# RWKV products over all 128 rows, adaLN weights as the moving operand, and shared accumulator buffers in a hybrid trunk kernel

## The chip, the core and the metric

The kernel runs on one core of a Trainium2 chip. A core has a matrix engine (TensorE, "PE" in the profile), a vector engine (VectorE, "DVE"), a scalar engine (ScalarE, "ACT"), a general engine (GpSimd, "POOL") and a queue engine that issues transfers (SyncE, "SP"). Each engine carries out its own instructions in order, and engines wait for each other through semaphores. Matmuls write to PSUM, which has eight banks, each 512 float32 values in each of 128 rows; everything else lies in SBUF. The metric is device time in microseconds (us). A comparison uses the median of several runs.

## What is computed

Two layers with shared weights go over 1,024 latent tokens and 256 context tokens of width 1,024. Three parts matter here.

```
mod = silu(c) @ w_ada[l] + b_ada[l]         # adaLN: 6 x 1024 columns per layer, for c and for c_ctx
h   = rmsnorm(x) * (1 + scale) + shift
...
w_raw = w0 + tanh(wd) @ w2                  # RWKV, per direction d; the two inputs are 64 wide
a     = sigmoid(a0 + ad @ a2)
S     = S * w_t + (S @ -kk_t) (kk_t * a_t) + v_t k_t      # scan over time, 8 heads of 64, two directions
y_t   = S @ r_t
```

The first layer runs attention and the RWKV scan as parallel head groups, the second a Fourier mixing; both end in a gated MLP with a width-3 convolution.

## The kernel before

Everything is float32. Large products split both operands in a high and a low part and add three products (L144 to L146); small ones run in plain float32, which PE carries out as two rows in the trace for each matmul.

The program goes through: the first adaLN blocks and norm, projections and attention, the RWKV part, the output product, the first MLP, the Fourier layer, and the second MLP. The change concerns the RWKV part and the adaLN products.

**RWKV.** The scan is chunked: 64 tokens a chunk, 256 tokens (4 chunks) a round for each direction, five rounds (four for the latent tokens, one for the context). A round has two halves of four heads. A half has four units, one for each direction `d` and pair of heads `pp_`. `unit_values` makes a unit's decays, keys and masks: two `lora` products (L789), then a chain through ACT, POOL and DVE. `unit_products` makes its 64-by-64 matrices (`G_ps`, L926) and transposes (`fl_ps`, L782). `half_prep` alternates the two, so that the products of a unit come behind the values of the next. `inverses` turns the triangular matrices of a whole round into inverses in 31 dependent steps on DVE (L978, L982). `corrections` applies them: `mq_ps` (L1018), `gv_ps` (L1023), `ms_ps` (L1030), `tb_ps` (L1036). `chains` carries the state over four chunks (`ch`, `y_ps`). `post` normalizes the result.

In `mq_ps` and `ms_ps` a matmul uses 32 rows and 32 columns of the array, in `gv_ps` 64 and 64, in `lora_ps` 64 rows and 128 columns. All other products of the part use all 128 rows. The operands stand on the rows that belong to the direction, and nothing is read on the others.

**adaLN.** `ada_steps` makes the first four blocks of 512 columns at the start: the vector is the stationary operand (32 columns, of which 2 hold data), the weights move, and four column quarters of the array (`ps[32 * q:...]`) take four parts of the sum; a second small product with `sel` (L202) adds the quarters and turns the row into columns. The other 10,240 columns are made by `ada_columns` in the RWKV part: the weights are the stationary operand, 128 by 128, and the vector moves with 2 columns (L239), eight matmuls for 128 columns, 80 such groups.

**PSUM in the RWKV part.** Two banks for the state chain `c0`, `c1`, two for `y0`, `y1`, two under the tag `t` for the corrections, two under the tag `g` for preparation, adaLN and `post` (`ps_g`).

**Order.** The function `run` interleaves generators by numbers: `A1` to `A5` say how many adaLN steps go into each phase of a round. The order on each engine is then settled by a scheduler when the program is built, so that instructions stand earlier or later than they are written where no dependence holds them.

Of the kernel before, what the change touches and what calls it, by code (L numbers as in the profile page):

```python
# [30 lines left out]
C = 64  # L31
QB = 6
# [66 lines left out]
def hybrid_step(ctx: ExitStack, tc: tile.TileContext, i: dict, o: dict):  # L99
# [77 lines left out]
    def ada_steps(l, j, wp, pp, tag, nb, kn, wb, sb):  # L177

        part, k1 = j // 2, j % 2 * 4
        ps = pp.tile([128, 512], F32, tag=tag, bufs=nb, name="ada_ps")  # L180
        for k0 in range(0, KD, kn):
            w = wp.tile([128, kn, 512], F32, tag="ada_w", bufs=wb, name="ada_w")
            ada_load[0] = nc.sync.dma_start(
                out=w,
                in_=i["w_ada"][l, k0 * 128:(k0 + kn) * 128, j * 512:(j + 1) * 512].rearrange(
                    "(k p) c -> p k c", p=128
                ),
            )
            for k in range(kn):
                q = (k0 + k) % 4  # L190
                nc.tensor.matmul(
                    ps[32 * q:32 * q + 32], lhsT=csil[:, k0 + k, :], rhs=w[:, k, :],
                    start=(k0 < 4), stop=(k0 >= 4),
                )
            if (k0 + kn) % 2 == 0:
                yield
        mp = wp.tile([128, 4, 128], F32, tag="ada_mp", bufs=sb, name="ada_mp")
        nc.scalar.copy(mp.rearrange("p k c -> p (k c)"), ps)
        yield
        ps = pp.tile([128, 4, 2], F32, tag=tag, bufs=nb, name="ada_ps2")  # L200
        for e in range(4):
            nc.tensor.matmul(ps[:, e, :], lhsT=mp[:, e, :], rhs=sel, start=True, stop=True)  # L202
        bc = lambda t: t.unsqueeze(1).to_broadcast([128, 2, 4])
        m = modc[l][:, part, :, k1:k1 + 4]
        nc.vector.tensor_tensor(
            out=m, in0=ps.rearrange("p k c -> p c k"), in1=bc(bcol[:, l, 4 * j:4 * j + 4]), op=ALU.add
        )
        gi = {1: 0, 2: 1, 4: 2, 5: 3}.get(part)
        if gi is not None:
            nc.vector.scalar_tensor_tensor(  # L210
                out=m, in0=m, scalar=1.0 if part in (1, 4) else 0.0, in1=bc(gcol[:, l, gi, k1:k1 + 4]),
                op0=ALU.add, op1=ALU.mult,
            )
        yield
        if part in (2, 5) and k1:
# [10 lines left out]

    def ada_columns(parts, wp, wb, ps_tile):

        for l, part in parts:
            m = modc[l][:, part]  # L230
            for k1 in range(KD):
                c0 = part * D + k1 * 128
                w = wp.tile([128, KD, 128], F32, tag="ada_c", bufs=wb, name="ada_c")
                nc.sync.dma_start(
                    out=w, in_=i["w_ada"][l, :, c0:c0 + 128].rearrange("(k p) c -> p k c", p=128)
                )
                ps = ps_tile()
                for k in range(KD):
                    nc.tensor.matmul(ps, lhsT=w[:, k, :], rhs=csil[:, k, 0:2], start=(k == 0), stop=(k == KD - 1))  # L239
                nc.scalar.activation(  # L240
                    m[:, :, k1], ps, AF.Identity, bias=bcol[:, l, part * KD + k1:part * KD + k1 + 1]
                )
                if k1 == KD - 1:
                    gi = {1: 0, 2: 1, 4: 2, 5: 3}.get(part)
                    if gi is not None:
                        nc.vector.scalar_tensor_tensor(
                            out=m, in0=m, scalar=1.0 if part in (1, 4) else 0.0,
                            in1=gcol[:, l, gi].unsqueeze(1).to_broadcast([128, 2, KD]), op0=ALU.add, op1=ALU.mult,
                        )
                    if part in (2, 5):  # L250
                        ps = ps_tile([16, 128])
                        nc.tensor.transpose(ps, m.rearrange("p c k -> p (c k)"), ident)
                        row = wp.tile([16, 128], F32, tag="ada_row", bufs=1, name="ada_row")
                        nc.scalar.copy(row, ps)
                        nc.gpsimd.dma_start(out=mod_d[l][part // 3].rearrange("c (k p) -> (c k) p", p=128), in_=row)
                yield
# [110 lines left out]
    with ExitStack() as st:  # L367
# [11 lines left out]
        with ExitStack() as st2:  # L379
# [3 lines left out]
            for _ in ada_blocks([(0, j) for j in (2, 3, 0, 1)], xp, pp, "t", 3, 2, 8, 1):  # L383
                pass
# [315 lines left out]
    with ExitStack() as st:  # L700
# [10 lines left out]
        PG = [pool(st_d, "pg", space=PSUM, side="right"), "g"]  # L711
# [28 lines left out]
        A1, A2, A3, A4, A5 = 5, 2, 3, 2, 8  # L740
# [14 lines left out]
        for t_ in bds + tzs:  # L755
# [12 lines left out]
        def ps_g(shape, name):  # L768
            return PG[0].tile(shape, F32, tag=PG[1], bufs=2, name=name)

# [14 lines left out]
        def lora(H, pp_, d, which, out):  # L785
# [4 lines left out]
                ps, lhsT=H["w"][HS[d], which, pp_ * 128:pp_ * 128 + 128], rhs=H["src"][HS[d], which, :],  # L790
# [4 lines left out]
        def half_new(n):  # L795
# [7 lines left out]
            H["w"] = ep.tile([128, 2, 256], F32, tag="w2", bufs=1, name="w2")  # L803
            for e, nm in enumerate(("rwkv_w2", "rwkv_a2")):
                for d in range(2):
                    nc.sync.dma_start(out=H["w"][HS[d], e, :], in_=i[nm][0, d, :, hf * 256:(hf + 1) * 256])
# [143 lines left out]
        def half_prep(R, H):  # L950
            H["src"] = R["src"]
            last = None
            for d, pp_ in UNITS:
# [1012 lines left out]
```

## Time and profile before

| | |
|---|---|
| median of 3 runs | 3950.23 us (3940.7 to 3959.45) |
| profiled execution | 3953.97 us, its span 3952.2 us |
| mean granted PE clock | 0.905 |
| RWKV part, about 700 to 1720 us of the span | PE busy 912 of 1020 us |
| memory traffic | 75 GB/s over the span |

How to read it: a row of a group names the line, the engine, the operation and its tiles (out<-in), the array's rows and columns in use (32*32), the moving operand's shape, the count, the busy time in us and the mean of one in ns, and then the idle time before them with what ended it. Busy spans of matmuls overlap, since a matmul starts before the one ahead has drained; so how often PE can start one is read from rows in order of time. PEclk is the share of the full PE clock that was granted.

### The profile page before, as it was taken

How to read it: one execution, taken by the hardware profiler on the slowest of the kernel's cores; microseconds unless marked ns; L12 is line 12 of the kernel's file. 1: busy time of each engine (PE TensorE's matmuls, PEld its weight loads, DVE VectorE, ACT ScalarE, POOL GpSimd, SP SyncE). 2: the span in 40 equal slices, each digit the busy share in tenths (PEclk: the TensorE clock that was granted, in tenths of full speed). 3: DMA queues.
4: the chain of work that ended last, by engine and by line, in shares of the span. 5: the costliest groups of instructions: out<-in, count | busy, mean ns of one | idle time of the engine just before them, and what ended most of it. 6: DMA issues, size and time to landing. Idle time of an engine off the chain costs nothing.

```text
span 3952.2 us, 54932 instructions
## 1 busy us (share of the span) xinstructions
PE 3702.0 (94%) x21512; PEld 3137.2 (79%) x21512; DVE 1945.5 (49%) x3685; ACT 1351.6 (34%) x2867; POOL 713.2 (18%) x1180
## 2 busy tenths in 40 slices
PE   7999997789999999789999999999887999999998
PEld 5888886578888878678888888888766888888886
DVE  4377666454444544566444444445655244444445
ACT  4266566533333333245321211212444321112121
POOL 3111111533333243224200000002233000000002
PEclk8999999568686757699999999999898999999999
DMA  6232312223332222144411111111541111111103
GB/s 215 85 100 77 99 65 66 78 78 96 96 100 83 83 81 68 44 144 123 126 40 40 38 34 37 43 38 60 191 125 54 38 38 38 38 40 40 39 30 125
DMA packets 368724, 299.42 MB, mean 76 GB/s; under 512 B 52939, under 2 KB 321067, under 8 KB 368465
## 3 DMA queue, kind: packets, MB, share of 16 engines
q1 hardware_dynamic: 304112, 235.81, 19.7%
q0 software_dynamic: 15952, 40.46, 3.0%
q10 hardware_dynamic: 48400, 19.65, 2.0%
q8 instruction: 169, 2.77, 0.3%
q14 instruction: 91, 0.74, 0.1%
HBM read 239.55 MB, written 58.33 MB: 75 GB/s over the span
## 4 chain that ended last, share of the span: by engine, by line
PE 82%; DVE 5%; DMA 3%; ACT 2%; POOL 2%; issue 2%; ACTq 0%; DVEq 0%; SPq 0%; POOLq 0%
PE a_ps L145 10%; PE a_ps L146 10%; PE a_ps L144 10%; PE b_ps L145 5%; PE b_ps L144 5%; PE b_ps L146 5%; PE ada_ps L239 4%; PE G_ps L926 3%; PE tb_ps L1036 3%; PE f_ps L144 2%; PE f_ps L146 2%; PE f_ps L145 2%; PE pv_ps L590 2%; PE sc_ps L554 2%; PE lora_ps L789 2%
## 5 line engine op out<-in xcount | busy, mean ns | idle before, releaser
L144 PE MATMUL a_ps<-hh,f_hi 128*128 128x512 f32 (+1 forms) x2144 | 761.4, 356 | 18.4 <-ACT f_hi L139 14.8
L145 PE MATMUL a_ps<-hl,f_hi 128*128 128x512 f32 (+1 forms) x2144 | 762.1, 356 | 3.2 <-POOL hl L342 3.2
L146 PE MATMUL a_ps<-hh,f_lo 128*128 128x512 f32 (+1 forms) x2144 | 760.8, 355 | 0.2 <-DVE f_lo L140 0.2
L1381 DVE TENSOR_TENSOR acc<-b_ps,acc 128x512 f32<-128x512 f32 x400 | 270.4, 689 | 405.9 <-PE b_ps L146 405.8
L144 PEld LDWEIGHTS a_ps<-hh,f_hi 128*128 128x128 f32 x2144 | 404.4, 189 | 82.7 <-ACT f_hi L139 15.4
L145 PEld LDWEIGHTS a_ps<-hl,f_hi 128*128 128x128 f32 x2144 | 404.3, 189 | 68.6 <-POOL hl L342 5.2
L146 PEld LDWEIGHTS a_ps<-hh,f_lo 128*128 128x128 f32 x2144 | 404.9, 189 | 63.0 <-DVE f_lo L140 0.9
L145 PE MATMUL b_ps<-d_lo,mh 128*128 128x512 f32 x880 | 349.1, 397 | 0.0
L146 PE MATMUL b_ps<-d_hi,ml 128*128 128x512 f32 x880 | 347.6, 395 | 0.0
L144 PE MATMUL b_ps<-d_hi,mh 128*128 128x512 f32 x880 | 342.1, 397 | 3.6 <-DVE acc L1381 3.1
L1327 POOL MEMSET gp<- 128x1 f32 x44 | 4.3, 98 | 1571.3 <-DVE cv L1346 1571.3
L140 DVE TENSOR_TENSOR f_lo<-f_raw,f_hi 128x512 fp32r<-128x512 f32 x176 | 114.3, 690 | 308.1 <-ACT f_hi L139 305.7
L239 PEld LDWEIGHTS ada_ps<-csil,ada_c 128*128 128x128 f32 x1280 | 218.9, 264 | 22.7 <-ACT th L793 8.5
L239 PE MATMUL ada_ps<-csil,ada_c 128*128 128x2 f32 x1280 | 223.3, 303 | 3.5 <-DMA ada_c<-in_w_ada 2.4
L139 ACT CAST d_hi<-d_raw 128x512 fp32r<-128x512 f32 x88 | 54.5, 621 | 488.5 <-PE b_ps L146 474.9
L144 PEld LDWEIGHTS b_ps<-d_hi,mh 128*128 128x128 f32 x880 | 165.8, 188 | 45.0 <-DVE acc L1381 4.6
L144 PE MATMUL f_ps<-hh,w_hi 128*128 128x512 f32 (+1 forms) x552 | 198.6, 360 | 0.5 <-ACT nk L478 0.5
L146 PEld LDWEIGHTS b_ps<-d_hi,ml 128*128 128x128 f32 x880 | 165.4, 188 | 40.7
L146 PE MATMUL f_ps<-hh,w_lo 128*128 128x512 f32 (+1 forms) x552 | 197.4, 358 | 0.0
L145 PE MATMUL f_ps<-hl,w_hi 128*128 128x512 f32 (+1 forms) x552 | 197.4, 358 | 0.0
L145 PEld LDWEIGHTS b_ps<-d_lo,mh 128*128 128x128 f32 x880 | 165.5, 188 | 37.4
L1338 ACT COPY gp<-a_ps 128x512 f32<-128x512 f32 (+1 forms) x134 | 68.0, 507 | 338.7 <-PE a_ps L146 338.7
(566 smaller groups left out, 6993.6 us busy)
## 6 DMA issues: line engine op xcount, KB each, us to landing
f_raw<-in_w_ffn_in SPq DMA_DIRECT2D x176, 256.0 KB, 3.2
ada_c<-in_w_ada SPq DMA_DIRECT2D x80, 512.0 KB, 4.0
d_raw<-in_w_ffn_out SPq DMA_DIRECT2D x88, 256.0 KB, 2.9
nx<-x_d SPq DMA_DIRECT2D x24, 512.0 KB, 4.6
w_raw<-in_w_in_even SPq DMA_DIRECT2D x23, 512.0 KB, 4.1
rx<-x_d SPq DMA_DIRECT2D x20, 512.0 KB, 7.0
ada_w<-in_w_ada SPq DMA_DIRECT2D x16, 512.0 KB, 8.8
fb_d<-fsh POOLq DMA_DIRECT2D x15, 512.0 KB, 3.1
```

Of the source, the lines that this page charges most:

```text
L140: nc.vector.tensor_tensor(out=lo, in0=src, in1=hi, op=ALU.subtract)
L144: nc.tensor.matmul(ps, lhsT=a[0], rhs=b[0], start=first, stop=False)
L145: nc.tensor.matmul(ps, lhsT=a[0], rhs=b[1], start=False, stop=False)
L146: nc.tensor.matmul(ps, lhsT=a[1], rhs=b[0], start=False, stop=last)
L239: nc.tensor.matmul(ps, lhsT=w[:, k, :], rhs=csil[:, k, 0:2], start=(k == 0), stop=(k == KD - 1))
L554: nc.tensor.matmul(ps[:, :nn], lhsT=qs[:, m, a, :], rhs=ks[m][:, n0:n0 + nn], start=(a == 0), stop=(a == 1),)
L590: nc.tensor.matmul(pv, lhsT=wt[:, kb, :], rhs=vt[:, kb, :], start=(kb == 0), stop=(kb == nk // 128 - 1))
L789: nc.tensor.matmul(ps, lhsT=H["w"][HS[d], which, pp_ * 128:pp_ * 128 + 128], rhs=H["src"][HS[d], which, :], start=True, stop=True,)
L926: nc.tensor.matmul(ps[:, c, :], lhsT=bd[:, c, h, :], rhs=kr[:, c].rearrange("p a s -> p (a s)"), start=True, stop=True,)
L1036: nc.tensor.matmul(ps[:, e, h, :], lhsT=tz[:, c + e, h, :], rhs=g[:, c + e, h, 64:192], start=True, stop=True,)
L1338: nc.scalar.copy(gp[:, o0:o0 + n], up(ws, t0, n))
L1381: nc.vector.tensor_tensor(out=acc[j][:, cs], in0=ps, in1=acc[j][:, cs], op=ALU.add)
```

## The change

Four things change. (1) `lora`, `mq_ps`, `gv_ps` and `ms_ps` read all 128 rows; the rows that hold nothing of the direction are zero in one of the operands, in tiles that are zeroed once (`w2s`, `svs`, `mqs`), and `tz` is zeroed in part in each unit. (2) `ada_columns` is gone; all 12,288 columns go through `ada_steps`, in blocks of 256 columns, with loads of four 128-row parts. (3) `half_prep` makes the values of both directions and then the products of both. (4) The tag `t` is gone: corrections share the tag `g`, now of three banks, with preparation and `post`, and adaLN has one bank of its own. The numbers `A1` to `A5` are set for the new count of steps (five a block, 40 blocks).

```diff
-    def ada_steps(l, j, wp, pp, tag, nb, kn, wb, sb):
+    def ada_steps(l, j, wp, pp, tag, nb, wb, sb):
+        na = AW // 128
+        part, k1 = j * na // KD, j * na % KD
+        ps = pp.tile([128, AW], F32, tag=tag, bufs=nb, name="ada_ps")
+        for k0 in range(0, KD, 4):
+            w = wp.tile([128, 4, AW], F32, tag="ada_w", bufs=wb, name="ada_w")
...
+            for q in range(4):
                 nc.tensor.matmul(
+                    ps[32 * q:32 * q + 32], lhsT=csil[:, k0 + q, :], rhs=w[:, q, :], start=(k0 == 0), stop=(k0 > 0),
                 )
...
-    def ada_columns(parts, wp, wb, ps_tile):
...
-                for k in range(KD):
-                    nc.tensor.matmul(ps, lhsT=w[:, k, :], rhs=csil[:, k, 0:2], start=(k == 0), stop=(k == KD - 1))
...
-            for _ in ada_blocks([(0, j) for j in (2, 3, 0, 1)], xp, pp, "t", 3, 2, 8, 1):
+            for _ in ada_blocks([(0, j) for j in (4, 5, 6, 7, 0, 1, 2, 3)], xp, pp, "t", 3, 8, 1):
...
-        PG = [pool(st_d, "pg", space=PSUM, side="right"), "g"]
+        PG = [pool(st_d, "pg", space=PSUM, side="right"), 3]
...
-        A1, A2, A3, A4, A5 = 5, 2, 3, 2, 8
+        A1, A2, A3, A4, A5 = 18, 4, 6, 6, 16
...
+        w2s = ep.tile([128, 2, 2, 256], F32, name="w2s")
+        svs = [lt.tile([128, NCP, 128], F32, name=f"sv{j}") for j in range(2)]
+        mqs = [lt.tile([128, 8, 32], F32, name=f"mqs{d}") for d in range(2)]
+        for t_ in [w2s] + bds + tzs + svs + mqs:
             nc.gpsimd.memset(t_, 0.0)
...
-                ps, lhsT=H["w"][HS[d], which, pp_ * 128:pp_ * 128 + 128], rhs=H["src"][HS[d], which, :],
+                ps, lhsT=H["w"][:, d, which, pp_ * 128:pp_ * 128 + 128], rhs=H["src"][:, which, :],
...
-            for d, pp_ in UNITS:
-                tmp = unit_values(H, d, pp_)
-                yield
-                if last:
-                    unit_products(R, H, *last, seen)
+            for pp_ in range(2):
+                tmp = []
+                for d in range(2):
+                    tmp.append(unit_values(H, d, pp_))
                     yield
+                for d in range(2):
+                    unit_products(R, H, d, pp_, tmp[d], seen)
+                    yield
...
+                nc.gpsimd.memset(tv[sr, :, fr], 0.0)
...
-                ps = pp.tile([64, nn_, 32], F32, tag="t", bufs=2, name="mq_ps")
+                ps = ps_g([64, nn_, 32], "mq_ps")
...
-                    nc.tensor.matmul(ps[sr, n, :], lhsT=gv[fr, n, sr], rhs=tv[fr, n, fr], start=True, stop=True)
+                    nc.tensor.matmul(ps[:, n, :], lhsT=gv[:, n, 0:64], rhs=tv[:, n, fr], start=True, stop=True)
...
-                            pv[:, c, h, :], lhsT=g[64:128, c, h, 0:64], rhs=sv[:, c, HS[h]], start=True, stop=True
+                            pv[:, c, h, :], lhsT=g[:, c, h, 0:64], rhs=sv[:, c, HS[h]], start=True, stop=True
...
-                    nc.tensor.matmul(ps[sr, n, :], lhsT=tn[sr, :, n0 + n], rhs=qs[sr, n, :], start=True, stop=True)
+                    nc.tensor.matmul(ps[sr, n, :], lhsT=tn[:, :, n0 + n], rhs=qs[:, n, :], start=True, stop=True)
...
-        ada = ada_columns(
-            [(0, 2), (0, 3), (0, 4), (0, 5)] + [(1, a) for a in range(6)], ep, 2, lambda s=[128, 2]: ps_g(s, "ada_ps")
+        ada = ada_blocks(
+            [(0, j) for j in range(8, 24)] + [(1, j) for j in range(24)], ep, PG[0], "ada", 1, 2, 1
         )
...
-                PG[:] = [pp, "t"]
+                PG[:] = [pool(st, "pz", space=PSUM), 2]
```

The built programs show how this moves instructions. On PE, in the preparation ahead of the first inverses, the kernel before has one unit's `lora` products (L789), then the products of the unit ahead of it (`G_ps`), and no adaLN:

```order
L926 MATMUL G_ps<-kr,bd_7297 128x128 x8
L775 MATMUL bon_ps<-bonk,ta 128x2 x2
L782 MATMUL fl_ps<-ident,bkw 128x128 x4
L775 MATMUL kk_ps<-bones,sq 128x2 x2
L782 MATMUL fl_ps<-ident,v 128x128 x2
L782 MATMUL fl_ps<-ident,rsx 128x128 x2
L789 MATMUL lora_ps<-lo_in,w_7649 128x256 x2
L926 MATMUL G_ps<-kr,bd_7296 128x128 x8
```

At the same place the changed kernel (its lines are numbered anew: L760 is `lora`, L897 `G_ps`, L191 the adaLN product with moving weights, L200 the small one with `sel`) has the `lora` products of two units, then the products of the two, and adaLN between them:

```order
L760 MATMUL lora_ps<-lo_in,w2s 128x256 x2
L191 MATMUL ada_ps<-ada_w,csil 32x256 x4
L746 MATMUL kk_ps<-bones,sq 128x2 x2
L753 MATMUL fl_ps<-ident,v 128x128 x2
L200 MATMUL ada_ps_9922<-sel,ada_mp 128x2 x2
L191 MATMUL ada_ps<-ada_w,csil 32x256 x4
L753 MATMUL fl_ps<-ident,rsx 128x128 x2
L760 MATMUL lora_ps<-lo_in,w2s 128x256 x2
L191 MATMUL ada_ps<-ada_w,csil 32x256 x4
L200 MATMUL ada_ps_10002<-sel,ada_mp 128x2 x2
L191 MATMUL ada_ps<-ada_w,csil 32x256 x4
L897 MATMUL G_ps<-kr,bd_7351 128x128 x8
```

adaLN has moved forward: of its 40 blocks of 256 columns in the RWKV part, 21 stand on PE ahead of the first corrections, and all 40 ahead of the second round's. Before, 6 of 80 groups stood ahead of the first corrections, 26 ahead of the second round's, and the last ahead of the fifth round's.

On PE at the first corrections, the kernel before:

```order
L239 MATMUL ada_ps<-csil,ada_c 128x2 x16
L1018 MATMUL mq_ps<-tz_7298,G 32x32 x8
L1023 MATMUL gv_ps<-sv,G 64x64 x8
L926 MATMUL G_ps<-kr,bd_7296 128x128 x4
L1030 MATMUL ms_ps<-mqs,xn 32x32 x8
L926 MATMUL G_ps<-kr,bd_7296 128x128 x4
L775 MATMUL bon_ps<-bonk,ta 128x2 x2
L1036 MATMUL tb_ps<-G,tz_7298 64x128 x8
```

The changed kernel there (L988 is `mq_ps`, L993 `gv_ps`, L1000 `ms_ps`, L1006 `tb_ps`):

```order
L988 MATMUL mq_ps<-tz_7352,G 64x32 x8
L993 MATMUL gv_ps<-sv_7355,G 64x64 x8
L191 MATMUL ada_ps<-ada_w,csil 32x256 x8
L1000 MATMUL ms_ps<-mqs_7357,xn 32x32 x8
L200 MATMUL ada_ps_11389<-sel,ada_mp 128x2 x2
L1006 MATMUL tb_ps<-G,tz_7352 64x128 x8
```

`mq_ps` fills 64 columns of the array where it filled 32, and the work between the corrections is adaLN instead of a unit's products. Counted over PE's rows from the first `kk_ps` to the output product, the shape in use (rows and columns of the array) changes 500 times before and 363 times now.

On ACT at the program's start, the kernel before copies the adaLN sums (`ada_mp`) and squares the input tiles (`njk`) in this order:

```order
L198 COPY ada_mp<-ada_ps 128x512 x3
L295 ACTIVATE njk,nss<-nx 128x1024 x3
L198 COPY ada_mp<-ada_ps 128x512
L295 ACTIVATE njk,nss<-nx 128x1024 x3
```

The changed kernel (L196 is the copy, L262 the square):

```order
L196 COPY ada_mp<-ada_ps 128x256 x5
L262 ACTIVATE njk,nss<-nx 128x1024
L196 COPY ada_mp<-ada_ps 128x256
L262 ACTIVATE njk,nss<-nx 128x1024 x3
L196 COPY ada_mp<-ada_ps 128x256
L262 ACTIVATE njk,nss<-nx 128x1024 x3
L196 COPY ada_mp<-ada_ps 128x256
```

The last copy stands behind seven squares instead of three.

More of the change, by code (lines that the diff above doesn't have):

```diff
@@ L31 @@
 C = 64
+AW = 256
 QB = 6
@@ L175, in hybrid_step @@
     ada_load = [None]
-    def ada_steps(l, j, wp, pp, tag, nb, kn, wb, sb):
[L179 to L182, printed above, removed]
+    def ada_steps(l, j, wp, pp, tag, nb, wb, sb):
[4 more added lines that the diff above has]
+            w = wp.tile([128, 4, AW], F32, tag="ada_w", bufs=wb, name="ada_w")
@@ L183, in ada_steps @@
             ada_load[0] = nc.sync.dma_start(
                 out=w,
-                in_=i["w_ada"][l, k0 * 128:(k0 + kn) * 128, j * 512:(j + 1) * 512].rearrange(
-                    "(k p) c -> p k c", p=128
-                ),
-            )
-            for k in range(kn):
-                q = (k0 + k) % 4
+                in_=i["w_ada"][l, k0 * 128:(k0 + 4) * 128, j * AW:(j + 1) * AW].rearrange("(k p) c -> p k c", p=128),
+            )
+            for q in range(4):
                 nc.tensor.matmul(
-                    ps[32 * q:32 * q + 32], lhsT=csil[:, k0 + k, :], rhs=w[:, k, :],
-                    start=(k0 < 4), stop=(k0 >= 4),
-                )
@@ L201, in ada_steps @@
-        for e in range(4):
+        ps = pp.tile([128, na, 2], F32, tag=tag, bufs=nb, name="ada_ps2")
+        for e in range(na):
             nc.tensor.matmul(ps[:, e, :], lhsT=mp[:, e, :], rhs=sel, start=True, stop=True)
-        bc = lambda t: t.unsqueeze(1).to_broadcast([128, 2, 4])
-        m = modc[l][:, part, :, k1:k1 + 4]
+        bc = lambda t: t.unsqueeze(1).to_broadcast([128, 2, na])
+        m = modc[l][:, part, :, k1:k1 + na]
         nc.vector.tensor_tensor(
-            out=m, in0=ps.rearrange("p k c -> p c k"), in1=bc(bcol[:, l, 4 * j:4 * j + 4]), op=ALU.add
+            out=m, in0=ps.rearrange("p k c -> p c k"), in1=bc(bcol[:, l, na * j:na * j + na]), op=ALU.add
@@ L210, in ada_steps @@
             nc.vector.scalar_tensor_tensor(
-                out=m, in0=m, scalar=1.0 if part in (1, 4) else 0.0, in1=bc(gcol[:, l, gi, k1:k1 + 4]),
+                out=m, in0=m, scalar=1.0 if part in (1, 4) else 0.0, in1=bc(gcol[:, l, gi, k1:k1 + na]),
                 op0=ALU.add, op1=ALU.mult,
@@ L214, in ada_steps @@
         yield
-        if part in (2, 5) and k1:
+        if part in (2, 5) and k1 + na == KD:
             ps = pp.tile([16, 128], F32, tag=tag, bufs=nb, name="ada_ps3")
@@ L225, in ada_blocks @@
             yield from ada_steps(l, j, *a)
-    def ada_columns(parts, wp, wb, ps_tile):
[L229 to L237, printed above, removed]
-                for k in range(KD):
[L239 to L256, printed above, removed]
     def mod_cols(l, part):
@@ L768, in ps_g @@
         def ps_g(shape, name):
-            return PG[0].tile(shape, F32, tag=PG[1], bufs=2, name=name)
+            return PG[0].tile(shape, F32, tag="g", bufs=PG[1], name=name)
         def head_sums(src, wt, name):
```

35 lines of the change are left out of this document (14 added, 21 removed).

## The prediction

> **What bounds the kernel now.** I read the page first, then the busy time by stage, then PE's groups in the stage that the change touches.
>
> ```profile
> span 3952.2 us, 54932 instructions
> ...
> PE   7999997789999999789999999999887999999998
> ...
> PEclk8999999568686757699999999999898999999999
> ```
>
> In the 40 slices PE is busy nearly throughout. Its granted clock is not: from about 700 us to 1720 us, the RWKV part, it is five to eight tenths. Nothing else in the program that the change touches weighs as much. The stages of that part, in columns of us, busy time by engine with its count, granted clock, DMA share and GB/s:
>
> ```profile
> core 0: us, PE busy (x) PEld busy (x) DVE busy (x) ACT busy (x) POOL busy (x), PEclk, DMA share, GB/s
> 700.00:797.00 97.00, 73.12 (x320) 57.22 (x320) 44.56 (x94) 53.34 (x113) 52.23 (x78) 0.62 0.27 76
> 797.00:852.00 55.00, 44.94 (x216) 39.76 (x217) 38.46 (x86) 19.98 (x42) 23.41 (x33) 0.51 0.33 96
> 852.00:999.00 147.00, 141.39 (x1236) 125.97 (x1234) 52.14 (x139) 56.29 (x115) 44.40 (x66) 0.77 0.29 87
> 999.00:1050.00 51.00, 45.77 (x224) 42.04 (x223) 36.71 (x80) 16.86 (x36) 19.86 (x30) 0.50 0.41 119
> 1050.00:1180.00 130.00, 128.40 (x1219) 116.31 (x1220) 47.06 (x121) 54.16 (x110) 42.61 (x63) 0.84 0.31 90
> 1180.00:1235.00 55.00, 50.04 (x243) 45.96 (x243) 36.77 (x79) 18.14 (x39) 20.71 (x31) 0.50 0.38 110
> 1235.00:1360.00 125.00, 122.69 (x1156) 110.24 (x1155) 51.09 (x127) 48.09 (x100) 37.40 (x61) 0.81 0.25 71
> 1360.00:1425.00 65.00, 50.21 (x267) 42.49 (x267) 51.58 (x97) 20.57 (x44) 29.82 (x28) 0.53 0.36 102
> 1425.00:1590.00 165.00, 161.01 (x1252) 143.25 (x1253) 59.48 (x138) 58.95 (x122) 50.48 (x71) 0.72 0.22 65
> 1590.00:1642.00 52.00, 28.71 (x152) 21.49 (x152) 38.20 (x85) 10.02 (x23) 18.95 (x14) 0.51 0.19 59
> 1642.00:1720.00 78.00, 66.14 (x788) 59.36 (x785) 32.32 (x93) 30.26 (x66) 11.87 (x20) 0.85 0.26 82
> ```
>
> Two kinds alternate. The four long stretches from 852 to 1590 us (147, 130, 125 and 165 us) hold corrections, chains and preparation: PE is busy 96% or more, no other engine more than 42% (PEld is PE's own weight load). There PE sets the pace. The five short ones that begin at 797, 999, 1180, 1360 and 1590 us hold the inverses: DVE is busy 38.46 + 36.71 + 36.77 + 51.58 + 38.20 = 201.7 of 278 us, and the clock is at half. PE's groups over 700 to 1720 us that matter here, and the adaLN products in the five short stretches with their sum:
>
> ```profile
> L239 PE MATMUL ada_ps<-csil,ada_c 128*128 128x2 f32 x1280 | 223.3, 303 | 3.5 <-DMA ada_c<-in_w_ada 2.4 <-ACT sq_ps L1186 1.1
> ...
> L789 PE MATMUL lora_ps<-lo_in,w 64*128 64x256 f32 x160 | 73.8, 589 | 0.0
> ...
> L1023 PE MATMUL gv_ps<-sv,G 64*64 64x64 f32 x640 | 55.4, 247 | 0.1
> ...
> L1030 PE MATMUL ms_ps<-mqs,xn 32*32 32x32 f32 x640 | 44.6, 227 | 0.0
> L1018 PE MATMUL mq_ps<-tz,G 32*32 32x32 f32 x640 | 31.2, 202 | 1.2 <-POOL tz L1014 1.2
> ```
>
> ```profile
> sum 278.00, PE 101.96 PEld 100.48 DVE 0.00 ACT 8.71; mean PE 20.39 PEld 20.10 DVE 0.00 ACT 1.74
> ```
>
> adaLN is the largest group, though its moving operand has two columns: each matmul costs a weight load of 128 columns. PE's rows in order of time (start, length, the group), at the program's start and in the RWKV part:
>
> ```profile
> 16.18 1.05 PE L202 MATMUL ada_ps<-sel,ada_mp 128*128 128x2 f32 x8 [0.73 <-ACT ada_mp L198]
> 17.16 2.35 PE L191 MATMUL ada_ps<-ada_w,csil 128*32 128x512 f32 x16
> ```
>
> ```profile
> 1447.60 0.69 PE L1018 MATMUL mq_ps<-tz,G 32*32 32x32 f32 x16
> 1448.21 0.44 PE L782 MATMUL fl_ps<-ident,v 128*128 128x128 f32 x2
> 1448.58 1.14 PE L1023 MATMUL gv_ps<-sv,G 64*64 64x64 f32 x16
> ...
> 1462.80 3.58 PE L239 MATMUL ada_ps<-csil,ada_c 128*128 128x2 f32 x16
> ...
> 1486.84 1.95 PE L239 MATMUL ada_ps<-csil,ada_c 128*128 128x2 f32 x16
> ```
>
> The same 16 rows of adaLN take 3.58 us at half clock and 1.95 us at full clock: what PE does in the RWKV part nearly doubles with the clock.
>
> **The change part by part.** The sum is made against the profiled execution, 3953.97 us (span 3952.2); the median of the runs shown, 3950.23, is 3.7 lower, and the difference is carried over as it is.
>
> *adaLN, what goes.* 223.3 us of PE time. Of it 102.0 lie in the five short stretches, 121.3 outside, where PE sets the pace; these 121.3 I count in full. In the short stretches DVE stays: they can shrink from 278 to no less than 201.7 us. I leave each 6 us of waits beside DVE, 232 us, so 46 of the 102 come out. Together -167.
>
> *adaLN, what comes.* The start shows the new form: a block of 512 columns takes 2.35 us and its `sel` rows 1.05. A block of 256 has half of both, 1.7 us; 40 blocks are 68 us at full clock, 136 at half. I take 90. By the order 21 of the 40 stand ahead of the first corrections, some 47 us of work; PE is free there for 97 - 73.1 = 24 us and 55 - 44.9 = 10 us. So 34 of the 90 hide, +56 (bounds 0 and 136).
>
> *Wider rows.* `lora` and `gv_ps` keep their columns, `ms_ps` too: no cost per row. `mq_ps` now loads 64 columns of weights. Its rows start (0.69 - 0.20)/15 = 33 ns apart; with 64 columns I give it the spacing of `gv_ps`, (1.14 - 0.22)/15 = 61 ns. 640 rows by 28 ns are 18 us at full clock, twice that at half: +20.
>
> *Changes of shape.* `mq_ps` begins at 1447.60, its 16th row by that spacing at 1448.10, and `fl_ps` with another shape not before 1448.21, though it waits for nothing: 0.08 us beyond the spacing. The order has 500 changes of shape before and 363 after: 137 by about 0.1 us, -14 (bounds 0 and -20).
>
> *The clock.* These two stretches decide what drives it:
>
> ```profile
> 1460.00:1480.00 20.00, 20.00 (x134) 17.80 (x133) 4.89 (x13) 4.18 (x9) 3.56 (x5) 0.50 0.21 60
> 1660.00:1680.00 20.00, 20.00 (x260) 18.88 (x259) 7.60 (x26) 5.29 (x12) 3.72 (x7) 0.88 0.08 23
> ```
>
> PE is busy all 20 us in both, yet the clock is 0.50 and 0.88. The first holds 22 adaLN rows, which stream two columns each, and products on 32 and 64 rows; the second holds no adaLN. The trace's clock records change only at steps of 3.41 us, so I counted for each such step of the RWKV part (299) the columns that PE's rows stream, each weighted by the share of the 128 array rows in use. Where a step reaches 0.375 of what the full clock could stream, the next step has the full clock: right in 293 of 299. Without the weight the best bound is right in 275. So rows of zeros count as work. Of the 182 steps at half clock, 38 would pass with all rows counted: 130 us at half clock that become full and halve, -65. The bounds: 0, if the tally is chance, and -130, since a faster step also makes the next denser and adaLN's two-column rows leave the stretches that they thinned.
>
> The Trainium skill, "TensorE: Matmul & The Clock Gate", Part 1, says that the gate follows how busy PE has been over windows of about 3.4 us. The step length agrees with the trace; that busy PE suffices does not, by the row at 1460 us. By the page a PE that is busy already would gain nothing from wider rows, and the sum would lack the 65.
>
> *Units by two, shared PSUM.* A unit's products now come behind the values of both directions, so `lora` of the next pair waits on PE behind `G_ps` of this one; corrections wait for a bank until ACT or DVE has emptied what preparation wrote. With PE shorter, the chain of ACT, POOL and DVE shows in the long stretches. None of this is in the trace. Nearest: PE is not busy for 4% of the first long stretch and 25% of the preparation alone (700 to 797 us). The four long stretches, 567 us less most of the 121, should come to some 450; 4% more of it is 18, 21% more (25 less 4) is 95, and a third bank for preparation could give back 10. I take the near end, since in the long stretches several streams fill PE: +20 (bounds -10 and +95).
>
> *The rest.* At the start the last `ada_mp` copy on ACT waits for four more squares, and the packets are half as long: +2 (-1 to +6). Forty small clears on POOL lie in its idle time, as it is busy 44.4 of 147 us in the first long stretch; without that cover they would cost some 0.3 us each, 12 us. The MLPs, attention and Fourier layer are the same.
>
> Sum: -167 + 56 + 20 - 14 - 65 + 20 + 2 = -148 us. 3953.97 - 148 = 3806, and against the median 3950.23 - 148 = **3802 us**.
>
> **The rivals.** (a) *The clock stays where it is*, because streaming, not rows, was what the tally saw. For it: unweighted streaming is right in 275 of 299 steps too, and the short stretches stay thin. Without the 65 the time is 3867. (b) *The full clock holds in all long stretches.* For it: adaLN leaves rounds two to five by the order, and 20 us at 1660 without it had 0.88. Another 65 us come out, and `mq_ps` costs no more than 18: 3735. (c) *DVE, ACT and POOL take over as soon as PE is shorter*, the dear end of the units' term with the clock's gain hidden: 3802 + 75 + 65 = 3942, no difference. (d) *Slower: PE stands for adaLN's weights.* Forty-two loads stand ahead of the first corrections, with two buffers, on a PE that goes in order.
>
> ```profile
> DMA to landing us min/median/max: 3.7/4.0/5.0
> ```
>
> A load lands 4.0 us after its issue. If each is waited out alone, 42 by 4.4 us (with the 0.4 of issue) are 185 us, and the time is 3802 + 185 = 3987. It decides once more than 34 of the 42 are waited out in full. Against it: before, PE waited 2.4 us in all for these loads, and 42 loads two at a time need some 92 us, which fit the 150 us ahead of the corrections.
>
> One rule speaks against the wider rows. The Trainium skill, "TensorEngine Tiling (Array Packing)", "When to Use Tiling", gives up to four matmuls at once for 32 rows. The `mq_ps` row above shows none to lose: all eight stand on the same 32 rows, and start one after the other.
>
> **How the numbers follow.** The forecast has 0.55, (a) 0.18, (b) 0.17, (c) 0.05, (d) 0.05. A measurement of this kernel can tell about 0.5%, 20 us, from no change. Faster: 0.90 (the forecast, (a) and (b)), same 0.05 (c), slower 0.05 (d). The range takes in (a) and (b) and the unknown costs about them, not (c) and (d): 3715 to 3885. Beyond it lie (c) and (d), 0.10, and some 0.08 of a gain larger than (b).
>
> **What would show it.** The adaLN rows of PE should fall from 223 us to about 90, with nearly none after the second round's corrections. The granted clock in the long stretches should rise from 0.72 to 0.84 to about 0.9 while the short ones stay near 0.5. The long stretches should shrink by some 25 to 45 us each, the short ones by 10. A clock that stays at 0.8 would show (a). PE idle with DMA as releaser ahead of the first corrections would show (d); long idle times of PE ended by ACT or DVE in the long stretches, (c). The prediction is wrong if the inverses' stretches do not shrink, or if the preparation ahead of the first inverses grows by more than 40 us.

## The result and the profile after

The changed kernel takes 3835.51 us (median of 4 runs, 3830.16 to 3840.11) against 3953.27 for the kernel before on the same chip: a ratio of 0.971, 95% interval 0.968 to 0.973. That is 118 us less, where the prediction had 148 less. The profiled execution took 3833.54 us, its span 3831.7, at a mean granted clock of 0.945 (before 0.905).

The page of the changed kernel, its span and the 40 slices of PE and of its clock:

```profile
span 3831.7 us, 54213 instructions
...
PE   7999998789687585899999999998968999999997
...
PEclk9999999869898796899999999999998999999999
```

The RWKV part has gained clock (five to eight tenths before, six to nine now) and lost busy time: PE is at five to nine tenths there, where it was at seven to nine. The same by stage (columns as in the prediction; the short stretches of 35 to 54 us are the inverses, each from its first step on DVE to the first `mq_ps` on PE):

```profile
core 0: us, PE busy (x) PEld busy (x) DVE busy (x) ACT busy (x) POOL busy (x), PEclk, DMA share, GB/s
715.00:818.00 103.00, 81.73 (x567) 58.17 (x563) 47.40 (x118) 55.55 (x116) 52.76 (x78) 0.75 0.70 210
818.00:861.00 43.00, 34.01 (x210) 21.03 (x209) 33.77 (x90) 15.88 (x42) 15.23 (x21) 0.64 0.67 206
861.00:1005.00 144.00, 133.89 (x1458) 108.64 (x1459) 61.70 (x180) 67.76 (x138) 57.74 (x89) 0.94 0.58 178
1005.00:1041.00 36.00, 14.10 (x93) 10.89 (x92) 33.15 (x83) 10.50 (x21) 11.09 (x17) 0.69 0.17 53
1041.00:1150.00 109.00, 95.93 (x1072) 85.23 (x1072) 50.98 (x123) 55.48 (x108) 54.91 (x85) 0.95 0.19 59
1150.00:1185.00 35.00, 8.91 (x49) 8.33 (x48) 32.59 (x77) 9.62 (x18) 11.28 (x17) 0.62 0.08 23
1185.00:1295.00 110.00, 95.41 (x1066) 84.44 (x1066) 59.64 (x135) 54.48 (x105) 50.25 (x82) 0.93 0.13 37
1295.00:1349.00 54.00, 23.69 (x93) 17.76 (x94) 51.94 (x98) 14.36 (x29) 31.59 (x28) 0.59 0.24 70
1349.00:1469.00 120.00, 99.76 (x1053) 89.36 (x1051) 57.74 (x132) 57.16 (x111) 51.86 (x80) 0.90 0.07 21
1469.00:1512.00 43.00, 10.72 (x30) 6.70 (x30) 38.65 (x82) 3.71 (x9) 15.00 (x7) 0.50 0.17 55
```

The reader is to see three things. The long stretches run at 0.90 to 0.95 of the clock. In the second to fourth of them PE is busy only 83 to 88% (95.93 of 109 us, 99.76 of 120): it no longer sets the pace alone. And in the short ones PE is busy 8.91 of 35 us while DVE is busy 32.59: nothing that PE gives up there can shorten them.

PE's groups that the change touches, 700 to 1600 us (L191 the adaLN product, L200 the one with `sel`, L988 to L1000 the corrections):

```profile
L191 PE MATMUL ada_ps<-ada_w,csil 128*32 128x256 f32 x640 | 64.2, 472 | 29.9 <-DMA ada_w<-in_w_ada 22.4 <-DVE mod L203 5.1 <-DVE sc L842 1.2
...
L988 PE MATMUL mq_ps<-tz,G 128*64 128x32 f32 x640 | 46.3, 228 | 43.7 <-POOL tz L984 42.5 <-ACT G L914 0.8 <-POOL wcol L861 0.3
...
L200 PE MATMUL ada_ps<-sel,ada_mp 128*128 128x2 f32 x160 | 26.9, 273 | 5.0 <-ACT ada_mp L196 5.0
```

adaLN is 64.2 + 26.9 us on PE, and waits 22.4 us for its weights. The largest waits of PE in the part (us in total, times, the longest):

```profile
PE mq_ps L988 <- POOL tz L984: 42.5, 3, 15.6
PE fl_ps L753 <- DVE y L1161: 37.2, 4, 12.2
PE G_ps L897 <- ACT bd L884: 27.4, 8, 8.9
```

The first is not POOL's doing. POOL's row in order of time ahead of the third round's corrections, and PE's behind it:

```profile
1184.68 1.26 POOL L984 COPY tz<-xt 32x256 f32<-32x256 f32 x2 [20.47 <-DVE xt L957]
```

```profile
1185.33 1.91 PE L988 MATMUL mq_ps<-tz,G 128*64 128x32 f32 x16 [15.64 <-POOL tz L984]
```

POOL itself stood 20.47 us until DVE had the inverses ready. PE has run out of work, and waits for DVE's chain. The kernel before has no such wait: its `mq_ps` rows wait 1.2 us for `tz` in all, by the row in the prediction.

Durations by stage, worked out from the starts of the first rows (us; the first `kk_ps` begins the preparation; the stretches as above, so the inverses are cut narrower than the windows of the prediction, which reached on to where the clock rose):

| | before | changed | difference |
|---|---|---|---|
| start and attention, to the first `kk_ps` | 696.4 | 715.5 | +19.1 |
| preparation, to the first inverse step | 99.5 | 102.1 | +2.6 |
| five inverses | 44.6, 44.5, 41.0, 39.8, 43.0 | 43.3, 36.2, 35.1, 54.7, 43.6 | 0.0 |
| four long stretches | 158.9, 136.5, 146.5, 182.1 | 144.0, 109.0, 109.3, 119.3 | -142.5 |
| last round | 88.5 | 86.2 | -2.3 |
| all behind | 2230.7 | 2233.3 | +2.6 |

That the inverses have the same sum, 213.0 us, is chance. The second and third are 8.3 and 5.9 us shorter; the fourth is 14.9 longer, and DVE, which also does part of `post` there, is busy 52.60 us in it where it was 37.43.

### The profile page after: what moved, and what is told of

The parts are those of the page before. It is cut to its first block, busy times and chain, and to the rows that moved or that the text cites. A ratio compares the mean times of both kernels' runs of the same rounds, so it can differ in the third digit from the quotient of the medians.

```text
span 3831.7 us, 54213 instructions
## 1 busy us (share of the span) xinstructions
PE 3464.8 (90%) x21096; PEld 2892.1 (75%) x21096; DVE 1956.9 (51%) x3752; ACT 1344.8 (35%) x2831; POOL 735.4 (19%) x1225
## 4 chain that ended last, share of the span: by engine, by line
PE 76%; DVE 7%; DMA 5%; ACT 3%; issue 2%; POOL 2%; ACTq 0%; SPq 0%; DVEq 0%; POOLq 0%
PE a_ps L146 10%; PE a_ps L147 10%; PE a_ps L145 10%; PE b_ps L146 5%; PE b_ps L145 5%; PE b_ps L147 5%; PE f_ps L145 2%; PE f_ps L146 2%; PE f_ps L147 2%; PE pv_ps L557 2%; PE tb_ps L1006 2%; PE sc_ps L521 2%; PE G_ps L897 2%; DMA ada_w<-in_w_ada 1%; DVE x L951 1%
## 5 line engine op out<-in xcount | busy, mean ns | idle before, releaser
L145 PEld LDWEIGHTS a_ps<-hh,f_hi 128*128 128x128 f32 x2144 | 404.2, 189 | 83.7 <-ACT f_hi L140 16.2
L1328 DVE TENSOR_TENSOR md<-a_ps,cv 128x512 f32<-128x512 f32 (+1 forms) x134 | 79.5, 595 | 164.8 <-PE a_ps L147 100.3
L140 ACT CAST f_hi<-f_raw 128x512 fp32r<-128x512 f32 x176 | 101.2, 620 | 156.2 <-PE a_ps L146 147.5
```

Source lines behind the costliest of these rows:

```text
L140: nc.scalar.copy(hi, src)
L145: nc.tensor.matmul(ps, lhsT=a[0], rhs=b[0], start=first, stop=False)
L1328: nc.vector.tensor_tensor(out=md, in0=ps, in1=cv[:, o0:o0 + n], op=ALU.mult)
```

## The experiments

Each run is compared with the kernel before on its own chip; between runs on different chips I compare the ratios. An interval is 0.0013 to 0.0029 to each side, 5 to 11 us.

| run | median us | ratio to before (95%) |
|---|---|---|
| changed kernel | 3835.5 | 0.9706 (0.9677 to 0.9734) |
| rows narrow again | 3914.5 | 0.9908 (0.9891 to 0.9925) |
| before, with wide rows alone | 3896.7 | 0.9864 (0.9845 to 0.9883) |
| adaLN in its old form | 3918.2 | 0.9914 (0.9896 to 0.9932) |
| PSUM of before | 3805.6 | 0.9633 (0.9612 to 0.9654) |
| units alternating again | 3837.3 | 0.9713 (0.9695 to 0.9732) |
| adaLN held back, own bank | 3859.9 | 0.9768 (0.9749 to 0.9787) |
| start of before | 3825.7 | 0.9694 (0.9672 to 0.9717) |
| start and PSUM of before | 3793.5 | 0.9608 (0.9589 to 0.9627) |
| and units alternating | **3777.3** | 0.9555 (0.9536 to 0.9574) |
| the same with one ring of four banks | 3816.1 | 0.9649 (0.9635 to 0.9662) |
| changed kernel without adaLN's products | 3805.1 | 0.9629 (0.9601 to 0.9656) |

**Rows narrow again**, in the changed kernel: the four products read only the rows of the direction.

```diff
-    ps, lhsT=H["w"][:, d, which, ...], rhs=H["src"][:, which, :],
+    ps, lhsT=H["w"][HS[d], d, which, ...], rhs=H["src"][HS[d], which, :],
...
-    lhsT=gv[:, n, 0:64], rhs=tv[:, n, fr]
+    lhsT=gv[fr, n, 0:64], rhs=tv[fr, n, fr]
...
-    lhsT=g[:, c, h, 0:64], rhs=sv[:, c, HS[h]]
+    lhsT=g[64:128, c, h, 0:64], rhs=sv[64:128, c, HS[h]]
...
-    lhsT=tn[:, :, n0 + n], rhs=qs[:, n, :]
+    lhsT=tn[sr, :, n0 + n], rhs=qs[sr, n, :]
```

> The changed kernel, but lora, mq_ps, gv_ps and ms_ps read only the 64 or 32 rows that hold data (same columns, same zeroed tiles, same counts). If rows of zeros count as work for the clock: granted clock in the long stretches of the RWKV part falls by 0.1 or more, time 3865 to 3900 us. If rows do not count and only the changes of shape do (some 130 more by 0.1 us): clock unchanged, 3835 to 3850 us.

It is 79 us slower than the changed kernel, above both ranges: rows count, and for more than was expected. The granted clock in the four long stretches is 0.84, 0.85, 0.78 and 0.84, against 0.94, 0.95, 0.93 and 0.90. Counted over the RWKV part, 145 of 282 clock steps of 3.41 us are at half clock, against 88 of 257 with wide rows. The columns streamed are the same in both. The changes of shape rise too, to 497 from 363, so this run alone does not part the two; but 57 more steps at half clock can cost up to 97 us by themselves.

**Before with wide rows alone**: the same four products and their zeroed tiles in the kernel before; besides, only the tiles `xn` and `si` move to other buffers.

> The kernel before, with the wide rows alone (adaLN columns, PSUM and the order of units as before). If rows count for the clock: 3880 to 3925 us (the prediction's -65 for the clock, -14 for changes of shape, +20 for mq_ps), clock over the RWKV part up from 0.69 by 0.05 to 0.1. If they do not: 3950 to 3975 us, clock unchanged.

It gains 1.36%, 54 us, and 130 of 280 steps are at half clock where 182 of 299 were. The shape in use changes 372 times in place of 500, so most of the fall in changes comes with the wide rows. From both sides the clock rises with the rows, at the same streamed columns; the next run, in which the shape never changes within a stretch, leaves the rows as the cause.

**Only products on PE.** Nothing of the model is computed. Dense stretches (128 rows, 128 columns of weights, 512 moving) alternate with other shapes.

```diff
+    go(full_rows, n)
+    for m, r in (
+        (rows_32, n), (rows_40, n), (rows_56, n), (rows_64, n), (zeros, n), (columns_32, n), (quarters, n),
+        (two_columns, 4 * n), (moving_64, 4 * n), (moving_64_rows_64, 4 * n),
+    ):
+        go(m, r)
+        go(full_rows, n)
```

> Only products on PE, nothing of the model is computed: stretches of 48 products (128 rows, 128 columns of weights, 512 moving columns) alternate with ten stretches of another shape, each issued back to back: 32, 40, 56 and 64 rows; 128 rows with zeros in both operands; 128 rows with 32 columns of weights; four column quarters of 32 with 256 moving columns; 128 by 128 with 2 moving columns; 128 by 128 with 64 moving columns; 64 rows with 64 moving columns. Theory A (streamed columns weighted by rows, bound 0.375): 32 and 40 rows (0.25 and 0.31) fall to half clock one step after their start, 56 and 64 rows (0.44 and 0.5) keep the full clock, zeros keep it, 32 columns and the quarters keep it, two moving columns fall to half, 64 rows with 64 columns fall. Theory B (streaming alone counts, as in the first rival of the prediction): 32 and 40 rows keep the full clock. Theory C (a busy PE is enough): all keep it. Theory D (the data count): zeros fall to half.

PE's rows in order of time (start, length; 32*128 is rows by columns of weights; the dense stretches between are left out but for one):

```profile
50.50 77.08 PE L122 MATMUL ps<-mv,wt 32*128 32x512 f32 x96
127.51 43.13 PE L119 MATMUL ps<-mv,wt 128*128 128x512 f32 x96
170.57 77.68 PE L125 MATMUL ps<-mv,wt 40*128 40x512 f32 x96
...
292.34 41.46 PE L128 MATMUL ps<-mv,wt 56*128 56x512 f32 x96
...
375.13 41.46 PE L131 MATMUL ps<-mv,wt 64*128 64x512 f32 x96
...
457.83 41.36 PE L134 MATMUL ps<-zm,zw 128*128 128x512 f32 x96
...
540.33 41.39 PE L140 MATMUL ps<-mv,wt 128*32 128x512 f32 x96
...
623.04 20.93 PE L144 MATMUL ps<-mv,wt 128*32 128x256 f32 x384
...
685.20 76.92 PE L147 MATMUL ps<-mv,wt 128*128 128x2 f32 x384
...
805.14 42.99 PE L150 MATMUL ps<-mv,wt 128*128 128x64 f32 x384
...
889.31 79.70 PE L153 MATMUL ps<-mv,wt 64*128 64x64 f32 x384
```

The granted clock inside the stretches of 32 and of 56 rows:

```profile
60.00:127.00 67.00, 67.00 (x80) 25.86 (x78) 0.00 (x0) 0.00 (x0) 0.50 0.00 0
...
293.00:333.00 40.00, 40.00 (x95) 17.46 (x94) 0.00 (x0) 0.00 (x0) 1.00 0.00 0
```

The same 96 rows of 512 columns take 41.5 us with 56 rows or more and 77 us with 40 or fewer; PE is busy throughout. So the bound lies between 40 and 56 of 128 rows, 0.31 and 0.44, which holds the 0.375 of the prediction's tally. Zeros count as data do, 32 columns of weights count as 128 do, and two moving columns do not keep the clock. Theory A holds in all that it names. The Trainium skill, "TensorE: Matmul & The Clock Gate", Part 1, has the clock follow how busy PE has been; a PE that is busy without a gap at 0.50 for 67 us speaks against that as the whole rule.

**adaLN in its old form**, in the changed kernel: `ada_columns` of before, on the bank of its own, with `A1` to `A5` of before.

> The changed kernel with adaLN in the RWKV part in its old form (weights stationary, two columns moving, 80 groups of eight), still with a bank of its own and so as early as before it. If the form of the adaLN products is the larger part of the gain: PE time of adaLN back to about 220 us, 3900 to 3970 us. If it is their place and the bank of their own: under 3870 us.

It is 83 us slower: that is what the new form of adaLN is worth there.

**Without adaLN's products**: loads, moving products and copies of the 40 blocks are left out, so this kernel does not compute the model; the products with `sel` stay, on zeros.

> The changed kernel with the loads, the moving products and the copies of the 40 adaLN blocks in the RWKV part left out; the small products with sel (on zeros) and what follows them stay. It measures what these 40 blocks still cost. The prediction had 90 us of PE for blocks and sel together, 34 of them hidden, so 56 on the path; without sel (about a third of it) some 40. Theory A (that stands, and the 22 us of waits for weights come on top): 3835.5 - 60, 3765 to 3785. Theory B (the blocks lie beside the start of the RWKV part, where PE has gaps): 3805 to 3825. Theory C (their rows hold the clock up in round one, so that without them the rest runs slower): 3825 to 3845.

It is 0.8% faster, 30 us: theory B. Of the 64.2 us of these products and 22.4 us of waits for weights, more than half lie beside other work. The five inverses still take 207.6 us in sum: without adaLN they hardly shrink further.

**PSUM of before**, in the changed kernel: two banks for the corrections, two for preparation, `post` and adaLN.

```diff
-        PG = [pool(st_d, "pg", space=PSUM, side="right"), 3]
+        PG = [pool(st_d, "pg", space=PSUM, side="right"), 2]
...
-                ps = ps_g([64, nn_, 32], "mq_ps")
+                ps = pp.tile([64, nn_, 32], F32, tag="g", bufs=2, name="mq_ps")
...
-            [(0, j) for j in range(8, 24)] + [(1, j) for j in range(24)], ep, PG[0], "ada", 1, 2, 1
+            [(0, j) for j in range(8, 24)] + [(1, j) for j in range(24)], ep, PG[0], "g", 2, 2, 1
```

> The changed kernel with the accumulator banks of before: two for the corrections, two for preparation, adaLN and post together. The scheduler then spreads adaLN over all rounds. If waits of PE for adaLN weights at the front (22 us of PE idle time put down to these loads, 45 us with the weight loads) cost more than the bank of its own gives: 3800 to 3830 us. If the two shared banks hold PE up in the rounds: 3845 to 3890 us.

It is 29 us faster than the changed kernel (0.9633 against 0.9706). The order changes too: 5, 15, 25, 33 and 40 of the 40 adaLN blocks stand ahead of the first corrections of the five rounds, against 21 and then all. So either the banks or the place could be the reason. (Tiles take the buffers of one tag in turn, in the order in which they are written; such a set is called a ring below.)

**adaLN held back, on its own bank**: the banks of the changed kernel, and nearly the places of the run above, counted ahead of the first corrections. The vector is copied anew in each round, with zero times the inverses added.

```diff
+                cr = ep.tile([128, KD, 32], F32, tag="csr", bufs=1, name="csr")
+                nc.gpsimd.tensor_scalar(out=cr, in0=R[q]["xn"][:, 0:8, :], scalar1=0.0, scalar2=None, op0=ALU.mult)
+                nc.gpsimd.tensor_tensor(out=cr, in0=cr, in1=csil, op=ALU.add)
```

> The changed kernel with its PSUM pools as they are (adaLN has a bank of its own), but the adaLN blocks of a round are held back until the inverses of that round are done: the vector that they multiply is copied anew by GpSimd from a tile that depends on the inverses (plus zero times their result). By the built order 5, 15, 25, 35 and 40 of the 40 blocks now stand ahead of the first corrections of rounds 1 to 5, as in the run with the PSUM of before (5, 15, 25, 33, 40), against 21, 40, 40, 40, 40 in the changed kernel. Theory A (what that run gained, some 30 us, came from the place of the adaLN blocks: ahead of the first corrections they run at a low clock and wait for loads): 3800 to 3815. Theory B (it came from the banks themselves: corrections and preparation no longer wait for each other's banks): 3830 to 3845.

Neither range: 25 us slower than the changed kernel (0.9768 against 0.9706). Fewer blocks ahead of the first corrections are not the gain by themselves; in these banks holding them back is a loss. PE stands 49.8 us for the inverses (42.5 in the changed kernel), and most of the blocks now lie in the long stretches, which take 525 us in place of 482. It does not part the banks from the place cleanly: of adaLN's moving products 28.9 us lie beside the inverses with the PSUM of before, and none here. The last run below parts them better.

**Units alternating again**, in the changed kernel: `half_prep` of before.

> The changed kernel with only the order of the units put back: the products of a unit stand behind the values of the next again; PSUM, adaLN and the wide rows stay as changed. Theory A (the pair order delays the first preparation: kk to inverses grew by 6.6 us, and lora of the next pair waits behind G of this one): the time falls by 5 to 15 us from 3835.5, to 3820 to 3830, and the stretch from the first kk_ps to the first inverse goes back towards 100 us. Theory B (with the other streams on PE the order of the units is free): within 5 us of 3835.5. Theory C (by two is better, since the shapes change less): slower, 3840 to 3855.

No difference: theory B.

**Start of before**, in the changed kernel: the first four blocks in 512 columns, with loads of two parts.

```diff
-            for _ in ada_blocks([(0, j) for j in (4, 5, 6, 7, 0, 1, 2, 3)], xp, pp, "t", 3, 8, 1):
+            for _ in ada_blocks([(0, j) for j in (2, 3, 0, 1)], xp, pp, "t", 3, 8, 1, 512, 2):
```

> The changed kernel with the four adaLN blocks at the program's start in the form of before (512 columns, loads of two 128-row parts, the order 2, 3, 0, 1). Theory A (the eight smaller blocks at the start cost the 6 us there, and the later tiles of the projections and attention another 6 by the moved order): 3823 to 3830, with the first n_ps at 38 us and the last ya_ps at 696. Theory B (only the start itself): 3828 to 3831, ya_ps at 702. Theory C (the attention hides it): within 3 us of 3835.5.

Theory A by its signs: the first `n_ps` is at 37.7 us (44.2 in the changed kernel), the last `ya_ps` at 695.1 (708.7). In the trace the first `kk_ps` comes 13.9 us earlier, but the end only 5.7, since the first preparation gives 8 us back. By the medians it is 10 us, by the ratios 5, which is within the interval. The changed kernel's start shows where the time was: a block of 256 columns takes nearly what one of 512 took (1.93 against 2.35 us). The same 16 rows take 1.07 us in the RWKV part:

```profile
28.43 1.93 PE L191 MATMUL ada_ps<-ada_w,csil 128*32 128x256 f32 x16
35.50 1.01 PE L200 MATMUL ada_ps<-sel,ada_mp 128*128 128x2 f32 x4 [5.14 <-ACT ada_mp L196]
...
928.04 1.07 PE L191 MATMUL ada_ps<-ada_w,csil 128*32 128x256 f32 x16
```

The reason is the clock. At the start four quarters of 256 columns follow each other every 427 ns (from 14.75 us on), at 928.04 us every 216 ns. So the start of the changed kernel runs at half clock; the first record of a full clock in its trace is at 56.1 us, in the kernel before at 16.2 us, and in this run at 15.2. In all seven traces of kernels that start with blocks of 256 columns it comes between 52.6 and 56.1 us, in the six with blocks of 512 between 15.2 and 27.0. (The view of the granted clock shows 1.00 where no record precedes; the spacing of the rows shows that it was half.) The late copy on ACT is no part of it: the kernel before has it too.

```profile
35.95 1.87 PE L202 MATMUL ada_ps<-sel,ada_mp 128*128 128x2 f32 x8 [5.61 <-ACT ada_mp L198]
```

Counted with a quarter of the weight, as at the end of this document, blocks of 256 columns stream about 0.25 of what the full clock could (1,024 columns in 3.42 us from one block to the next), below the 0.375 of the prediction's tally. That fits, but no run tests the count by itself.

**Start and PSUM of before**, together.

> The changed kernel with the start in the form of before and the PSUM pools of before, both together: wide rows, adaLN with moving weights in the RWKV part, and units by two stay. If the two gains are independent (30 us and 6 to 12 us): 3790 to 3800, faster than both kernels. If the start's gain is hidden by attention: 3803 to 3808.

3793.5: the two add up, within the interval.

**And units alternating as well**: of the change there stay the wide rows and adaLN's new form.

> The start and the PSUM pools of before, and the units alternating as before: of the change there stay the wide rows and adaLN with moving weights in the RWKV part. Theory A (the order of the units is free, as the run that put it back in the changed kernel showed): within 8 us of 3793.5, the time with the start and the PSUM pools of before and units by two. Theory B (with corrections on banks of their own the pair order fills PE better during the inverses): 3803 to 3820. Theory C (the first preparation gains from alternating): 3780 to 3787.

3777.3 us, the fastest: 4.5% less than before. Nearest is theory C, and the time lies 3 us below its range. The first preparation takes 97.8 us in place of 103.7, as theory C has it, but the first long stretch also shrinks, from 117.6 to 111.7. Against the run with units by two, it is 0.5% (21 us by the ratios, 16 by the medians): what was free in the shared ring costs something once corrections have banks of their own.

**One ring of four banks**: the fastest version, the two pairs of banks made one ring.

```diff
-        PG = [pool(st_d, "pg", space=PSUM, side="right"), 2]
+        PG = [pool(st_d, "pg", space=PSUM, side="right"), 4]
...
-                ps = pp.tile([64, nn_, 32], F32, tag="g", bufs=2, name="mq_ps")
+                ps = ps_g([64, nn_, 32], "mq_ps")
...
-            [(0, j) for j in range(8, 24)] + [(1, j) for j in range(24)], ep, PG[0], "g", 2, 2, 1
+            [(0, j) for j in range(8, 24)] + [(1, j) for j in range(24)], ep, PG[0], "g", 4, 2, 1
```

> The fastest version so far (wide rows and adaLN with moving weights on the start, the order of units and the PSUM pools of before, 3777.3) with one edit: the two pairs of banks become one ring of four that corrections, preparation, post and adaLN take in turn. The number of banks and the places of the adaLN blocks stay (8, 18, 28, 38 and 44 of 48 ahead of the corrections of the five rounds, against 9, 19, 29, 37 and 44). Theory A (what the change's PSUM cost is that corrections and preparation stand in one ring, so that one's bank waits until the other's has been emptied): 3805 to 3830, with PE standing longer ahead of the first corrections and of G. Theory B (a ring of four is as good as two pairs; the cost came from adaLN's bank of its own, which lets the blocks run ahead to where the clock is low): 3770 to 3785. Theory C (one ring of four is freer than two pairs): below 3770.

Theory A: 0.9649 against 0.9555, 37 us. There are as many banks, and adaLN is in nearly the same places (beside the inverses 26.1 us of its moving products, against 33.6). The second round's inverses and the long stretch behind them, in the fastest version and, in the second fence, with one ring:

```profile
947.00:993.00 46.00, 32.66 (x181) 21.14 (x180) 39.85 (x95) 18.86 (x36) 20.96 (x30) 0.66 0.55 171
993.00:1095.00 102.00, 98.61 (x1143) 86.52 (x1142) 45.74 (x122) 50.79 (x100) 44.11 (x72) 0.94 0.32 97
```

```profile
969.00:1008.00 39.00, 18.21 (x116) 11.45 (x116) 36.19 (x86) 13.95 (x28) 16.99 (x24) 0.69 0.55 168
1008.00:1122.00 114.00, 106.33 (x1206) 93.46 (x1207) 50.76 (x131) 55.57 (x108) 50.54 (x78) 0.93 0.32 98
```

PE's waits for the inverses, in the same order:

```profile
PE mq_ps L991 <- POOL tz L987: 10.4, 2, 5.9
```

```profile
PE mq_ps L991 <- POOL tz L987: 43.1, 3, 15.0
```

With pairs PE works 32.66 us during the inverses, with one ring 18.21, then stands, and the work follows in the long stretch. PE's rows say which work: ahead of the second round's first corrections stand the `G_ps` of 19 units with pairs, of 17 with one ring (304 and 272 rows, 16 to a unit). PE's waits for `rsx` (preparation) and `y` (`post`) grow too, from 25.7 to 48.1 and from 19.4 to 33.3 us. The reading that fits: a tile of the next half's preparation that is written behind a correction takes its bank behind it too, and the correction waits for DVE. The Trainium skill, "Perfetto Trace Analysis", "Matmuls", wants independent groups to rotate through different banks. Here they do in both versions; what decides here is whether a group that waits stands in the same rotation.

## Why the prediction was right, and where it was not

The sign, the main mechanism and the range held (3835.5 lies in 3715 to 3885); 30 us of the gain were missing. Below, the prediction's terms stand beside the steps from version to version (ratios times 3953.27). The split holds for this order of steps: units by two cost nothing in the changed kernel's own banks.

| step | predicted | measured |
|---|---|---|
| rows (+20 for `mq_ps`, -65 clock, -14 shapes): before to wide rows alone | -59 | -54 |
| adaLN (-167 + 56): to the fastest version | -111 | -122 |
| units by two (0.9555 to 0.9608) and shared PSUM (0.9608 to 0.9694) | +20 | +21 and +34 |
| start (0.9694 to 0.9706) | +2 | +5 |
| sum | -148 | -116 |

*Clock: right.* With wide rows alone 52 fewer steps are at half clock, where 38 were forecast. `mq_ps` now starts every 57 ns ((1.07 - 0.22)/15, from 16 rows that follow each other at 1048 us), forecast 61. In the long stretches of the changed kernel the clock is 0.90 to 0.95, forecast 0.9; in the short ones it is 0.50 to 0.69, forecast near 0.5. The -14 for shapes belongs to this step, since the changes fall to 372 with the wide rows alone; its size was not measured apart.

*adaLN: the amount right, the place in part wrong.* The new rows take 91 us (forecast 90), and none come behind the second round's corrections. But 46 us were to come out of the inverses' stretches, some 10 from each. The second and third gave 8.3 and 5.9, the first 1.3, the last nothing, and the fourth grew by 14.9: in sum nothing. (They are cut narrower here than in the prediction; what its wider windows gave besides is counted in the long stretches.) I had priced them by DVE's busy share and took PE's 102 us there for part of the length. Their floor is a chain on DVE; for the changed kernel's third round, the 62 steps alone:

```profile
L951 DVE TENSOR_TENSOR x<-x,tm 128x31 f32<-128x31 f32 (+15 forms) x31 | 12.3, 398 | 0.8
L947 DVE TENSOR_TENSOR tm<-nn,x 128x31 f32<-128x31 f32 (+15 forms) x31 | 12.0, 386 | 0.9
```

24.3 us of steps, and DVE's other work between them, make 32.59 us of the 35 with PE nearly idle. The prediction named inverses that do not shrink as a sign that would show it wrong, and in this step, by the sum, it was. The long stretches gave 142.5 us in all, within the 100 to 180 of four times 25 to 45, but unevenly: 14.9 in the first, 62.8 in the last. Their clock lies between the forecast and the second rival's full clock.

*Units by two and shared PSUM: the cause named, its place and size off.* This is the term that missed most: 55 us, not 20, within its bounds of -10 to +95. The 11 us that adaLN gave beyond its term, no more than the noise of one such step, hid part of the miss; that is luck. I took the near end because several streams fill PE in the long stretches. The wait came where I had not looked, ahead of the corrections, where PE stands until the inverses are done, and, as the run with one ring bears out, preparation cannot pass them in the ring.

*The start: the clock overlooked.* Half the columns were to cost half the time (1.7 us a block). At full clock they do (1.07 us, and 0.61 for `sel` at 909.16 us). But the start of the changed kernel runs at half clock, and a block takes 1.93 + 1.01 there: the term was made for the copy on ACT and left the clock out.

*The rivals.* (a) fell with the clock run. (d), PE standing for weights, is 22.4 us in place of 185. (c), that others take over, is true in part: PE is busy 83 to 88% in the later long stretches. The changes of shape were not measured apart, and whether the 25 us by which holding adaLN back lost come from its single bank or from its place in the long stretches stays open.

## What to carry to other kernels

Count PE's work for the clock as streamed columns times rows in use: where small products leave a busy PE at half clock, zero rows that cost no column can be worth more than the work they add. Cutting blocks smaller can leave PE at half clock, as at this kernel's start. Before removing PE work from a stretch, ask whether a chain on another engine sets its length, by the dependent steps and not by the busy share. Give a stage that waits for a chain its own PSUM buffers, so that work written behind it can pass.

## What the runs showed of the hardware

The clock went to half with 40 rows streaming without a gap and stayed full with 56; 128 rows of zeros kept it full as 128 rows of data did. Four column quarters really run at once: 384 rows of 256 columns took 20.93 us, 54 ns each, where 96 rows of 512 on the whole array took 41.4, 431 ns each; four times as fast per column. For the clock the four seem to count as one: with a quarter of the weight for them the tally is right in 251 of the changed kernel's 257 steps, with the full weight in 233 (with narrow rows 266 and 233 of 282). That is a count over traces; no run tested it by itself.
